# First layer's feed-forward: half-size products for the latent tokens, output products in groups of two, context part first at the end

## The chip, the cores and the metric

The kernel runs on one core of one Trainium2 chip. The metric is the device time of one execution in microseconds (us). A core has TensorE (PE in the rows; PEld is its weight load), VectorE (DVE), ScalarE (ACT), GpSimd (POOL) and the queue engine SP, which issues most DMAs. Each engine executes its instructions in the order in which they stand in its program.

## The reference, cut to what matters

Two layers over 512 latent tokens and 256 context tokens of width 1024, in float32. The change lies in the feed-forward of the first layer (`layer == 0`), which works on both kinds of tokens:

```python
def _swiglu(h, w_in, w_out):
    g, u = jnp.split(h @ w_in, 2, axis=-1)
    return (jax.nn.silu(g) * u) @ w_out
...
x = x + g1 * y
x = x + g2 * _swiglu(_rmsnorm(x, norm_w[layer, 1]) * (1.0 + sc2) + sh2, ffn_w_in[layer], ffn_w_out[layer])
if not last:
    ctx = ctx + cg1 * yc
    ctx = ctx + cg2 * _swiglu(_rmsnorm(ctx, norm_w[layer, 1]) * (1.0 + csc2) + csh2, ffn_w_in[layer], ffn_w_out[layer])
```

The hidden width is 2816, so `w_in` is 1024 x 5632 (2816 gate columns, 2816 up columns) and `w_out` is 2816 x 1024. The modulation vectors (`sc2`, `sh2`, `g2` and so on) come from `silu(c) @ ada_w[layer]`.

## The kernel before

**Numbers.** Every float32 product is made of three products of rounded halves. A value is split into a high part (a cast on ACT) and a low part (value minus high part, a subtraction on DVE), and a product is high x high + high x low + low x high, all added up in one PSUM bank. So each weight tile costs one ACT cast (`wh`, `xh`) and one DVE subtraction (`wl`, `xl`), and each activation tile likewise.

**Layout.** Activations lie with features on partitions and tokens along the free axis: columns 0 to 255 are context (`CTX`), 256 to 767 latent (`LAT`); `LA` and `LB` are the two halves of LAT. `xt` is the residual stream, `g0h`/`g0l` the normed input of the first feed-forward in its two parts, `h1h`/`h1l` the normed input of the second layer's attention.

**The first feed-forward** (`op_ffn`). The 2816 hidden features are 22 tiles of 128, taken two at a time (`pr`, 11 pairs). For a tile, gate and up columns are each multiplied with LAT in one go (matmuls of 512 columns into `pg` and `pu`) and with CTX (matmuls of 256 columns): 2 x 8 x 3 matmuls of either width. ACT takes the silu, DVE multiplies (`hfull`), ACT and DVE split the result (`fh`, `fl`). After pairs 2, 4, 6, 8 an output product (`outproj`, `pf`) follows over the four tiles before them; a last one takes the remaining six tiles, LAT first and then CTX, each followed by its norm. Each output bank is added to `xt` by one DVE instruction.

**The second feed-forward** (`op_ffn_seven`) works on latent tokens alone, and already uses seven half-size products instead of eight: the 1024 input features are cut in two halves, the gate/up columns are the second direction, the 512 tokens the third, and sums and differences of blocks are multiplied. It needs weight sums on DVE (`ws`), split like weights, forms of the activations (`hT`), and five DVE additions and subtractions of 256 columns per tile (`u`, `hfull`, `sq` from `pu`). Its rows show what such work costs.

**What sets the order.** `Flow` runs streams (generators) by modelled engine times and so writes out one program order. The streams are the main one (products, one after the other), `Weights` (loads of weights through three buffers `wr`, splits), norms, and `ada`: the modulation of later stages, which DVE computes as `acc` instructions of 1024 columns (two for each of 8 row blocks, or one where the context vector isn't needed). `op_ada` starts one such task after each of pairs 1 to 7; the first, (0, 40), gives the factors that every output product of this feed-forward needs. The row blocks of `ada_w` come through a ring of six buffers `aw`.

**Around it.** Ahead of the feed-forward stands the output product of the mixers (`op_out`, `pf` from `mh`, `ml`): 8 LAT products, the LAT norm, 8 CTX products, the CTX norm. A norm is `nsum` (PE sums the squares), `v` (DVE), a power on POOL, `nbc` (PE), then 8 multiplications on DVE with ACT and DVE or POOL behind them. After it stands the key projection of the attention (`pt`), latent chunks first, context chunks last.

Of the kernel before, what the change touches and what calls it, by code (L numbers as in the profile page):

```python
# [143 lines left out]
def kernel(ctx, tc, x, c, cx, c_ctx, ada_w, ada_b, norm_w, ffn_w_in, ffn_w_out, ab_w_in,  # L144
# [334 lines left out]
    F1 = {}  # L479


    class Weights:
# [8 lines left out]
        def plan(self, specs):  # L491

            for sp in specs:
                i = len(self.todo)
                if sp[0] in ("seven", "eight"):
# [39 lines left out]
        def seven(self, i, job):  # L535


            yield lambda: self.asked > job[1] and "pool" in F1
# [15 lines left out]
            def sums():  # L554
                return F1["pool"].tile([P, KT, P], F32, tag="ws", name=nm("ws"), bufs=3)

            x = [F1["pool"].tile([P, 12, P], F32R, tag=t, name=nm(t), bufs=2) for t in ("xh", "xl")]
# [16 lines left out]
            split("u", [t[:, 8:12] for t in x], u[:, 4:8])  # L574
            self.freed += 2
            self.ask()
            yield
# [4 lines left out]
            split("y", whl(), y)  # L582

# [154 lines left out]
    def ada_open():  # L738
        ada_ring["ctx"] = ExitStack()
        pool_ = ada_ring["ctx"].enter_context(tc.tile_pool(name="aw", bufs=6))  # L740
# [4 lines left out]
        for _ in range(6):  # L745
# [709 lines left out]
    def mixers_end():  # L1455
# [3 lines left out]
        ada_open()  # L1459

# [37 lines left out]
    op_out(ab_w_out[0], mixed, 0, 2, (LAT, CTX), op_norm(0, 1, "g0"), (32, 24))  # L1498
# [3 lines left out]
    def halves_ps(t):  # L1502
        return [t[:, 0:512], t[:, 512:1024]]

    def op_ffn(l, name, parts, ends, ada, then, last=None):

        acts = {}
        x_ = lambda: ready[name]

        def inproj(pr, ada):  # L1510
            def gen():
                th, tl = big([P, 2, NT], F32R, "fh"), big([P, 2, NT], F32R, "fl")
                acts[pr] = th, tl
                def evac(t, part, pg, pu):
                    a, b, mc = part
                    n = b - a
                    sg = t3("sq")
                    act.activation(sg[:, 0:n], pg[:, 0:n], AF.Silu)
                    fu = t3("hfull")
                    dve.tensor_tensor(fu[:, 0:n], pu[:, 0:n], sg[:, 0:n], ALU.mult)  # L1520
                    act.copy(th[:, t, a:b], fu[:, 0:n])
                    dve.tensor_tensor(tl[:, t, a:b], fu[:, 0:n], f(th[:, t, a:b]), ALU.subtract)

                for t in range(2):
                    first = pr == 0 and t == 0
                    u, ps = [], []
                    for i, part in enumerate(ends if first else parts):
                        a, b, mc = part
                        if first:
                            yield lambda: a in ready[name + "done"]  # L1530
                        for j in range(2):
                            if len(u) <= j:
                                u += yield from W.take(1)
                                ps.append([bank("pg") for _ in range(2)] if j == 0 else halves_ps(psum2("pu")))
                            yield from steps(ps[j][i][:, 0:b - a], pairs_feat(u[j], 0, *x_(), a, b), cut=24)
                            if part is (ends if first else parts)[-1]:
                                W.give(1)
                            if j:
                                evac(t, part, ps[0][i], ps[1][i])
                            flow.cur.t = 0.0  # L1540
                            yield
            specs = []
# [655 lines left out]
```

## Time and profile before

| | |
|---|---|
| median of the runs shown | 1776.29 us |
| profiled execution, its own time | 1777.82 us |
| span of the profiled execution | 1776.0 us |
| PE busy | 1721.4 us (97%) |
| DVE busy | 1136.9 us (64%) |
| ACT busy | 685.5 us (39%) |
| first feed-forward | about 545 to 1120 us of the span |
| second feed-forward | about 1400 to 1765 us of the span |

The time of the profiled execution is its span and 1.8 us around it. A busy PE is one with a matmul in its pipeline, so how quickly it works is read from the distance between the starts of matmuls. Durations of DVE instructions in the rows overlap those of their neighbours a little, so their cost in a row of instructions is also read from start to start.

### The profile page before, as it was taken

The numbers are of one execution on the slowest core, as the hardware profiler recorded it, in microseconds if no ns is written. First come the engines' busy times: TensorE is split into PE (matmuls) and PEld (weight loads), VectorE is DVE, ScalarE is ACT, GpSimd is POOL, SyncE is SP. The second block draws the span as 40 slices with busy tenths as digits, with TensorE's granted clock in tenths as the row PEclk, the third lists the DMA queues.
The fourth block names the chain that finished last, engine by engine and source line by source line (L and its number), as shares of the span: only waits on it lengthen the run. The fifth ranks groups of instructions, "written<-read, shape, count | busy, mean of one in ns | idle before, by whom it ended". The sixth has DMA issues, their size and how long they took to land.

```text
span 1776.0 us, 29522 instructions
## 1 busy us (share of the span) xinstructions
PE 1721.4 (97%) x11922; PEld 1528.9 (86%) x11922; DVE 1136.9 (64%) x2048; ACT 685.5 (39%) x1346; POOL 274.6 (15%) x271
## 2 busy tenths in 40 slices
PE   6899999999999999999999999898999999999998
PEld 5799899999878888888888888898666989999998
DVE  5845365756597376563544324869886687778785
ACT  4532344433325221212121123545776553444343
POOL 4211120201123000000000002426454300000000
PEclk8999899999999999999999999898999999999999
DMA  9511111011574264443542215322002623333335
GB/s 332 209 52 48 37 37 48 25 38 53 196 239 117 75 186 132 129 148 125 162 134 78 67 37 153 96 61 60 1 1 66 184 72 95 107 96 107 107 88 150
DMA packets 224556, 184.35 MB, mean 104 GB/s; under 512 B 7532, under 2 KB 206628, under 8 KB 224420
## 3 DMA queue, kind: packets, MB, share of 16 engines
q1 hardware_dynamic: 222468, 178.20, 32.9%
q10 hardware_dynamic: 1952, 4.27, 0.7%
q8 instruction: 94, 1.54, 0.4%
q14 instruction: 42, 0.34, 0.1%
HBM read 175.10 MB, written 7.34 MB: 103 GB/s over the span
## 4 chain that ended last, share of the span: by engine, by line
PE 84%; DVE 7%; ACT 3%; issue 3%; DMA 2%; POOL 1%; SPq 0%; POOLq 0%; ACTq 0%; DVEq 0%
PE pf L107 28%; PE pu L107 18%; PE pg L107 14%; PE pt L107 10%; PE sc L107 3%; PE ao L107 2%; PE mo L107 2%; PE atr L107 2%; PE ro L107 1%; DVE acc L107 1%; PE kv L107 1%; DVE wl L107 1%; PE me L107 1%; DMA wr<-in_ab_w_in_dram 1%; DVE hfull L107 1%
## 5 line engine op out<-in xcount | busy, mean ns | idle before, releaser
L107 ACT CAST wh<-wr 128x1024 fp32r<-128x1024 f32 (+1 forms) x186 | 188.2, 1012 | 345.7 <-PE pf L107 165.5
L107 DVE TENSOR_TENSOR wl<-wr,wh 128x1024 fp32r<-128x1024 f32 (+1 forms) x186 | 225.4, 1212 | 105.5 <-ACT wh L107 104.3
L107 POOL TENSOR_TENSOR nacc<-nacc,sq 128x256 f32<-128x256 f32 (+1 forms) x42 | 56.7, 1349 | 630.7 <-ACT sq L107 627.5
L107 DVE SCALAR_TENSOR_TENSOR xt<-pf,mod,xt 128x512 f32<-128x512 f32 (+1 forms) x160 | 97.7, 613 | 84.3 <-PE pf L107 83.8
L107 DVE TENSOR_TENSOR hfull<-pu,sq 128x512 f32<-128x512 f32 (+1 forms) x44 | 24.5, 557 | 149.9 <-PE pu L107 149.6
L107 PE MATMUL pf<-fh,wh 128*128 128x256 f32 (+1 forms) x352 | 119.3, 340 | 0.8 <-ACT wh L107 0.8
L107 PE MATMUL pf<-fl,wh 128*128 128x256 f32 (+1 forms) x352 | 118.5, 337 | 0.0
L107 PE MATMUL pf<-fh,wl 128*128 128x256 f32 (+1 forms) x352 | 118.0, 338 | 0.5 <-DVE wl L107 0.5
L107 PE MATMUL pf<-fu,wh 128*128 128x512 f32 (+1 forms) x448 | 116.2, 349 | 1.1 <-ACT fu L107 0.5
L107 PE MATMUL pu<-hT,wh 128*128 128x256 f32 x640 | 115.4, 280 | 0.0
L107 DVE SCALAR_TENSOR_TENSOR acc<-aw,cmod,acc 128x1024 f32<-128x1024 f32 x90 | 114.8, 1298 | 0.0
L107 PEld LDWEIGHTS pu<-hT,wh 128*128 128x128 f32 x640 | 97.8, 188 | 0.6 <-ACT hT L107 0.2
L107 PE MATMUL pu<-hT,wl 128*128 128x256 f32 x320 | 88.0, 281 | 1.4 <-DVE wl L107 1.4
L107 PE MATMUL pt<-wh,hh 128*128 128x256 f32 x288 | 84.2, 294 | 3.8 <-ACT hh L107 2.6
L107 PEld LDWEIGHTS pf<-fu,wh 128*128 128x128 f32 x448 | 76.8, 188 | 12.6 <-ACT fu L107 0.7
L107 PE MATMUL pt<-wl,hh 128*128 128x256 f32 x288 | 83.7, 292 | 0.0
L107 PE MATMUL pg<-g0h,wh 128*128 128x512 f32 (+1 forms) x220 | 82.1, 373 | 1.5 <-ACT sq L107 1.5
L107 POOL TENSOR_TENSOR aE<-aE,ast 128x512 f32<-128x512 f32 (+1 forms) x64 | 73.0, 1154 | 66.9 <-DVE ast L107 51.5
L107 PE MATMUL pg<-g0l,wh 128*128 128x512 f32 (+1 forms) x220 | 82.3, 374 | 0.0
L107 PE MATMUL pt<-wh,hl 128*128 128x256 f32 x288 | 82.2, 288 | 0.0
L107 PE MATMUL pu<-g0l,wh 128*128 128x512 f32 (+1 forms) x220 | 82.1, 373 | 0.0
L107 PE MATMUL pu<-g0h,wh 128*128 128x512 f32 (+1 forms) x220 | 81.9, 372 | 0.0
(382 smaller groups left out, 5169.2 us busy)
## 6 DMA issues: line engine op xcount, KB each, us to landing
wr<-in_ffn_w_in_dram SPq DMA_DIRECT2D x88, 512.0 KB, 3.9
aw<-in_ada_w_dram SPq DMA_DIRECT2D x84, 512.0 KB, 4.5
wr<-in_ab_w_in_dram SPq DMA_DIRECT2D x32, 512.0 KB, 4.3
wr<-in_ffn_w_out_dram SPq DMA_DIRECT2D x32, 512.0 KB, 4.7
wr<-in_ffn_w_out_dram SPq DMA_DIRECT2D x32, 384.0 KB, 3.6
wr<-in_ab_w_out_dram SPq DMA_DIRECT2D x16, 512.0 KB
wr<-in_attn_w_out_dram SPq DMA_DIRECT2D x16, 512.0 KB, 4.1
aw<-in_ada_w_dram SPq DMA_DIRECT2D x8, 768.0 KB
```

The lines of the kernel that those rows point to most:

```text
L107: r = fn(*a, **k)
```

## The change

The first feed-forward gets a function of its own, `op_ffn_first`.

- Its input product for the latent tokens is made of seven products of half size, as in the second layer; for the context tokens it stays as it was. Work goes by single tiles (`fi`, 22). The order in a tile is: b11, a context half, b21, t2, t3, n1, the other context half, n4, b22.
- The norm of LAT makes the forms that these products need (`norm_seven0`): b11 and b21 first, and t2, t3, n1, n4, b22 once the CTX part of the mixers' output product has been issued (`mixed`). The CTX norm starts after form n1.
- `Weights.seven` gets a third kind, "all", whose weights g, z, y and u are all 1024 wide; g and u go to a pool of their own (`F0`).
- Output products take two tiles each (nine groups of two, one of one, and the last of three). The last runs over CTX, LA, LB in turn, each with its norm behind it; the key and value projections behind it go by chunks 0, 1, 2 in place of 1, 2, 0.
- The `aw` ring holds three buffers in place of six, `ada` tasks start after tiles 0, 3, 6 and so on to 18, and the first has a shorter pause between its steps (1 us in place of 2, in `Flow`'s modelled time).

```diff
@@ Weights.seven
-            x = [F1["pool"].tile([P, 12, P], F32R, tag=t, name=nm(t), bufs=2) for t in ("xh", "xl")]
+            def xs_():
+                return [F["pool"].tile([P, F["rows"], P], F32R, tag=t, name=nm(t), bufs=2) for t in ("xh", "xl")]
+            x = xs_()
...
+            if job[2] == "all":
+                yield
+                yield spend((self.n_x, 1))
+                split("u", xs_(), u)
+                self.freed += 2
+                self.ask()
@@ ada_open
-        pool_ = ada_ring["ctx"].enter_context(tc.tile_pool(name="aw", bufs=6))
+        pool_ = ada_ring["ctx"].enter_context(tc.tile_pool(name="aw", bufs=3))
@@ norm_seven0
+        for q in range(4):
+            bb.append(big([P, 3, NL], F32, "bb"))
+            for k in range(2):
+                kk = 2 * q + k
+                dve.scalar_tensor_tensor(bb[q][:, k], xk(xt, kk, a, b), amod[0][:, 1, kk, 0:1], bcs, ALU.mult, ALU.mult)
+                act.activation(bb[q][:, k], bb[q][:, k], AF.Identity, bias=mod[0][:, 24 + kk, 0:1])
+            two(("b11", "b21")[q // 2], q % 2, bb[q][:, 0:2, 0:256])
+        done0.update(("b11", "b21"))
...
+        yield lambda: "mixed" in done0
+        for name in ORDER0[2:]:
+            for q, (b11, b21, b12, b22, t2) in enumerate(four):
+                if name == "t3":
+                    dve.tensor_tensor(b12, b12, b22, ALU.subtract)
+                if name == "n4":
+                    dve.tensor_tensor(b21, b21, t2, ALU.subtract)
+                two(name, q, {"t2": t2, "t3": b12, "n1": b11, "n4": b21, "b22": b22}[name])
+            done0.add(name)
+            yield
@@ op_ffn_first.inproj
+                product(bank_a, u["g"], 0, "b11")
+                act.copy(m1, bank_a)
...
+                if fi:
+                    bank_e = psum("pc", "mx")
+                    yield from context(0)
...
+                product(bank_a, u["g"], 4, "b21", start=False)
...
+                product(bank_b, u["z"], 0, "t2")
+                dve.tensor_tensor(u23[:, 0], bank_b, m1, ALU.subtract)
...
+                product(bank_d, u["y"], 0, "t3")
+                dve.tensor_tensor(u23[:, 1], bank_d, u23[:, 0], ALU.add)
...
+                product(bank_c, u["y"], 4, "n1")
+                W.give(1)
+                cc = t3("hfull")
+                dve.tensor_tensor(cc[:, 256:512], u23[:, 1], bank_c, ALU.subtract)
...
+                product(bank_d, u["u"], 4, "n4", start=False)
...
+                dve.tensor_tensor(cc[:, 0:256], bank_d, u23[:, 0], ALU.add)
...
+                product(bank_c, u["z"], 4, "b22", start=False)
+                W.give(1)
+                dve.tensor_tensor(m1, bank_c, u23[:, 0], ALU.subtract)
+                act.activation(m1, m1, AF.Silu)
+                dve.tensor_tensor(cc, cc, keep, ALU.mult)
+                act.copy(t[:, 0, NCX:NT], cc)
+                dve.tensor_tensor(t[:, 1, NCX:NT], cc, f(t[:, 0, NCX:NT]), ALU.subtract)
...
+            op(gen, [("all",) + columns(0, fi)])
+            if ada and fi % 3 == 0:
                 l_, t0 = ada.pop(0)
+                op_ada(l_, t0, on_pe=(), gap=5.0 if l_ else 1.0, cols=1 if l_ and t0 >= 16 else 2)
@@ op_ffn_first.outproj
             if end:
+                for part in (CTX, LA, LB):
                     op(lambda part=part: gen((part,)), specs)
                     then(part)
...
+        groups = {fi: (fi - 2, fi - 1) for fi in range(2, 12, 2)}
+        groups[11] = (10,)
+        groups.update((fi, (fi - 2, fi - 1)) for fi in range(13, 20, 2))
+        groups[NF - 1] = (NF - 3, NF - 2, NF - 1)
@@ op_tok, keys and values of the attention
-    op_tok(wat[:, D:D + 256], h1, (1, 2, 0), evac_nr(1, lambda c2: None if c2 == 0 else 2 * c2 - 2, post_k, kdone.add),
+    op_tok(wat[:, D:D + 256], h1, (0, 1, 2), evac_nr(1, lambda c2: None if c2 == 0 else 2 * c2 - 2, post_k, kdone.add),
```

Whole program, matmuls of the two products of the first feed-forward: before, 1584 of 512 columns (1056 of the input product, 528 of the output product) and 1584 of 256 columns (the same two parts); now, 456 of 512 columns and 3576 of 256 columns (2904 of the input product, 672 of the output product).

DVE, between the LAT norm and the first products of the feed-forward; `xt` adds a CTX output bank of the mixers, `bb` are the normed latent blocks and `g` the low parts of the forms. Before:

```order
L107 SCALAR_TENSOR_TENSOR g0l_5545<-hfull_5631,mod_173,g0h_5542 128x512
L107 SCALAR_TENSOR_TENSOR xt_4891<-pf_5804,mod_173,xt_4891 128x256
L107 TENSOR_TENSOR wl_5841<-wr_5796,wh_5839 128x1024
L107 SCALAR_TENSOR_TENSOR hfull_5640<-xt_4890,amod_175,nbc_5617 128x512
L107 SCALAR_TENSOR_TENSOR xt_4891<-pf_5845,mod_173,xt_4891 128x256
L107 TENSOR_TENSOR wl_5909<-wr_5802,wh_5907 128x1024
```

Now, at the same place:

```order
L107 SCALAR_TENSOR_TENSOR xt_4891<-pf_5823,mod_173,xt_4891 128x256
L107 TENSOR_TENSOR bb_5640<-bb_5640 128x2x256
L107 TENSOR_TENSOR wl_5911<-ws_5878,wh_5910 128x1024
L107 TENSOR_TENSOR wl_5927<-ws_5879,wh_5926 128x1024
L107 TENSOR_TENSOR bb_5632<-bb_5648,bb_5632 128x512
L107 TENSOR_TENSOR bb_5632<-bb_5632,bb_5648 128x2x256
L107 TENSOR_TENSOR g_907_5653<-bb_5648,g_905_5645 128x512
L107 SCALAR_TENSOR_TENSOR bb_5656<-xt_4891,amod_175,nbc_5627 128x512 x2
L107 TENSOR_TENSOR ws_6107<-wr_5805,wr_5957 128x512
L107 TENSOR_TENSOR ws_6107<-wr_5957 128x512
L107 TENSOR_TENSOR g_934_5856<-bb_5632,g_907_5653 128x512
```

Sums of blocks (`bb`), sums of weights (`ws`) and their splits stand there now, among the multiplications of the norm; the low part of the last quarter of b21 comes after them.

DVE, ahead of the first output product: `acc` belongs to the task (0, 40), `wl` from `wr` is the low part of the output weights, `xt` from `pf` the first addition. Before:

```order
L107 TENSOR_TENSOR fl_6425<-hfull_6622,fh_6424 128x512
L107 TENSOR_TENSOR wl_6656<-wr_6416,wh_6654 128x1024
L107 TENSOR_TENSOR hfull_6690<-pu_6595,sq_6688 128x256
L107 TENSOR_SCALAR acc_6714<-aw_6489,cmod 128x1024
L107 TENSOR_TENSOR wl_6710<-wr_6519,wh_6708 128x1024
L107 TENSOR_SCALAR acc_6716<-aw_6489,cmod 128x1024
L107 TENSOR_TENSOR fl_6425<-hfull_6690,fh_6424 128x256
L107 STREAM_TRANSPOSE row_6704<-row_6703 128x256
```

Now:

```order
L107 SCALAR_TENSOR_TENSOR acc_6115<-aw_6171,cmod,acc_6115 128x1024
L107 TENSOR_TENSOR hfull_6280<-pu_6228,u_981_6123 128x256
L107 TENSOR_TENSOR wl_6347<-ws_6283,wh_6346 128x1024
L107 TENSOR_TENSOR xl_6411<-wr_6246,xh_6410 128x1024
L107 SCALAR_TENSOR_TENSOR acc_6117<-aw_6171,cmod,acc_6117 128x1024
L107 TENSOR_TENSOR fu_6121<-sq_6350,fu_6121 128x256
L107 SCALAR_TENSOR_TENSOR acc_6115<-aw_6188,cmod,acc_6115 128x1024
L107 TENSOR_TENSOR keep_6122<-pu_6267,u_981_6123 128x256
L107 TENSOR_TENSOR wl_6434<-wr_6248,wh_6432 128x1024
```

The task (0, 40) stands among the splits of the second and third tile, and the low part of the first output weights (`wl_6434`) stands behind most of it.

PE at the start of the first output product, where `wl_6434` is read (`pu`, `pg`: banks of the tiles; `ada`: column sums of the finished `acc`). Before, the product of pairs 0 and 1, between the products of a later pair:

```order
L107 MATMUL pg_6560<-g0h_5544,wh_6412 128x256
L107 MATMUL pg_6560<-g0l_5547,wh_6412 128x256
L107 MATMUL pg_6560<-g0h_5544,wl_6414 128x256
L107 MATMUL pf_6720<-fh_5879,wh_6585 128x512
L107 MATMUL pf_6720<-fl_5880,wh_6585 128x512
L107 MATMUL pf_6720<-fh_5879,wl_6587 128x512
L107 MATMUL pu_6595<-g0ch_5918,wh_6515 128x256
```

Now, the product of tiles 0 and 1, among the products of the third tile (`pg` is its product with b11):

```order
L107 MATMUL pu_6451<-g_943_5905,wh_6346 128x256
L107 MATMUL pu_6451<-g_942_5900,wl_6347 128x256
L107 MATMUL pf_6541<-fu_5861,wh_6432 128x512 x2
L107 MATMUL pf_6541<-fu_5861,wl_6434 128x512
L107 MATMUL ada_6210<-acc_6115,ones 32x256 x4
L107 MATMUL pg_6358<-g_903_5637,xh_6263 128x256 x2
L107 MATMUL pg_6358<-g_903_5637,xl_6264 128x256
```

The first output product comes after two tiles in place of four, and the sums of the task (0, 40) stand right behind its first rows. Between the LAT norm's `nsum` and the row that reads `wl_6434` stand 432 matmuls of 256 columns, which are 144 of the mixers' CTX output product, 264 of the first two tiles and 24 of the third.

## Rows read from the trace of the kernel before

**Rows 1.** The page's part 1: busy us, share, instructions, by engine.
```profile
PE 1721.4 (97%) x11922; PEld 1528.9 (86%) x11922; DVE 1136.9 (64%) x2048; ACT 685.5 (39%) x1346; POOL 274.6 (15%) x271
```

**Rows 2.** The page's part 4: the chain that ended last, by engine.
```profile
PE 84%; DVE 7%; ACT 3%; issue 3%; DMA 2%; POOL 1%; SPq 0%; POOLq 0%; ACTq 0%; DVEq 0%
```

**Rows 3.** Windows, first and second feed-forward: length, busy by engine, clock, DMA share, GB/s.
```profile
545.00:1110.00 565.00, 562.67 (x3241) 485.96 (x3241) 287.38 (x369) 134.63 (x202) 19.52 (x17) 1.00 0.38 116
1500.00:1740.00 240.00, 238.89 (x1741) 225.08 (x1739) 189.21 (x286) 99.77 (x146) 0.00 (x0) 1.00 0.33 98
```

**Rows 4.** Timeline of PE, starts of matmuls of 512 and of 256 columns.
```profile
1080.17 0.40 PE L107 MATMUL pf<-fh,wh 128*128 128x512 f32 x1
...
1098.70 0.39 PE L107 MATMUL pf<-fh,wl 128*128 128x512 f32 x1
...
1108.97 0.28 PE L107 MATMUL pf<-fl,wh 128*128 128x256 f32 x1
...
1111.33 0.28 PE L107 MATMUL pf<-fh,wh 128*128 128x256 f32 x1
```

**Rows 5.** Timeline of DVE, instructions that stand close behind each other.
```profile
655.44 0.75 DVE L107 TENSOR_SCALAR acc<-aw,cmod 128x1024 f32<-128x1024 f32 x1
656.11 1.22 DVE L107 TENSOR_TENSOR wl<-wr,wh 128x1024 fp32r<-128x1024 f32 x1
...
671.40 2.47 DVE L107 SCALAR_TENSOR_TENSOR acc<-aw,cmod,acc 128x1024 f32<-128x1024 f32 x2
673.79 0.48 DVE L107 SCALAR_TENSOR_TENSOR xt<-pf,mod,xt 128x256 f32<-128x256 f32 x1
674.18 1.21 DVE L107 TENSOR_TENSOR wl<-wr,wh 128x1024 fp32r<-128x1024 f32 x1
...
1681.00 0.69 DVE L107 TENSOR_TENSOR xl<-wr,xh 128x512 fp32r<-128x512 f32 x1
1681.61 2.36 DVE L107 TENSOR_TENSOR wl<-ws,wh 128x1024 fp32r<-128x1024 f32 x2
1683.88 0.75 DVE L107 SCALAR_TENSOR_TENSOR xt<-pf,mod,xt 128x512 f32<-128x512 f32 x1
1684.54 0.68 DVE L107 TENSOR_TENSOR ws<-ws,wr 128x512 f32<-128x512 f32 x1
...
1704.21 0.41 DVE L107 TENSOR_TENSOR hfull<-pu,u 128x256 f32<-128x256 f32 x1
1704.55 0.41 DVE L107 TENSOR_TENSOR u<-pu,m 128x256 f32<-128x256 f32 x1
```

**Rows 6.** Timeline of PE and of DVE at the LAT norm ahead of the feed-forward.
```profile
529.73 1.05 PE L107 MATMUL nsum<-cst,nacc 128*128 128x1 f32 x8
...
534.78 0.15 DVE L107 TENSOR_SCALAR v<-nsum 128x4 f32<-128x4 f32 x1
```

**Rows 7.** Waits of PE, 525 to 580 us.
```profile
PE pf L107 <- DVE xt L107: 2.0, 2, 1.6
```

**Rows 8.** Windows: ahead of the first feed-forward, and at the second one's forms (columns as in rows 3).
```profile
534.80:557.40 22.60, 22.60 (x167) 20.71 (x166) 19.43 (x29) 14.56 (x23) 12.45 (x11) 1.00 0.71 201
1430.00:1440.00 10.00, 9.29 (x76) 8.86 (x75) 9.97 (x18) 8.26 (x17) 0.00 (x0) 1.00 0.01 2
```

**Rows 9.** Windows behind the first feed-forward (columns as in rows 3).
```profile
1120.00:1130.00 10.00, 8.01 (x52) 7.38 (x51) 5.72 (x9) 5.08 (x8) 6.04 (x6) 0.83 0.48 145
1130.00:1140.00 10.00, 7.75 (x51) 7.55 (x50) 8.50 (x21) 4.59 (x10) 1.64 (x1) 0.82 0.01 2
1140.00:1150.00 10.00, 9.67 (x69) 9.70 (x70) 7.36 (x11) 3.83 (x6) 4.18 (x3) 0.83 0.00 1
1150.00:1160.00 10.00, 10.00 (x87) 10.00 (x87) 7.86 (x14) 5.63 (x10) 1.65 (x1) 1.00 0.33 105
```

**Rows 10.** Waits of PE, 1116 to 1160 us.
```profile
PE pt L107 <- DVE sq L107: 2.6, 1, 2.6
```

**Rows 11.** DMA issues, 545 to 1110 us: count, KB, median us to landing.
```profile
aw<-in_ada_w_dram SPq DMA_DIRECT2D x50, 512.0 KB, 3.9
```

More of the change, by code (lines that the diff above doesn't have):

```diff
@@ L477, in spend @@
         return cond
-    F1 = {}
+    F0, F1 = {}, {}
     class Weights:
@@ L535, in seven @@
         def seven(self, i, job):
-            yield lambda: self.asked > job[1] and "pool" in F1
+            F = F0 if job[2] == "all" else F1
+            yield lambda: self.asked > job[1] and "pool" in F
             yield spend((self.n_x, 1))
@@ L744, in ada_open @@
         ada_ring["todo"] = ada_ring["plan"]
-        for _ in range(6):
+        for _ in range(3):
             ada_ask()
@@ L1459, in mixers_end @@
         ada_open()
+        F0["ctx"] = ExitStack()
+        F0["pool"] = F0["ctx"].enter_context(tc.tile_pool(name="f0", bufs=1))
+        F0["rows"], F0["sums"] = 8, 2
     op_do(mixers_end)
@@ L1497 @@
     mixed = lambda: (lambda k, a, b: mh[k // 2][:, k % 2, a:b], lambda k, a, b: ml[k // 2][:, k % 2, a:b])
[L1498 to L1505, printed above, removed]
-        acts = {}
-        x_ = lambda: ready[name]
-        def inproj(pr, ada):
-            def gen():
[L1512 to L1542, printed above, removed]
-            for t in range(2):
-                c0 = 256 * pr + P * t
-                specs += [wfeat(ffn_w_in[l, :, c:c + P]) for c in (c0, DFF + c0)]
-            op(gen, specs)
-            if ada and pr >= 1:
-                l_, t0 = ada.pop(0)
-                op_ada(l_, t0, on_pe=(), gap=5.0 if l_ else 2.0, cols=1 if l_ and t0 >= 16 else 2)
-        def outproj(prs):
-            nk = 2 * len(prs)
-            r0 = 256 * prs[0]
-            ncol = 256 if nk == 4 else P
-            end = prs[-1] == DFF // 256 - 1
-            bh = lambda k, a, b: acts[prs[k // 2]][0][:, k % 2, a:b]
-            bl = lambda k, a, b: acts[prs[k // 2]][1][:, k % 2, a:b]
-            specs = [(ffn_w_out[l, r0:r0 + P * nk, ncol * s:ncol * s + ncol], nk, ncol) for s in range(D // ncol)]
@@ new lines, in norm_ctx0, with norms0, run, columns @@
+    def norm_ctx0():
+        yield lambda: "n1" in done0
+        yield from norm_mod(0, 1, ctx0(0), ctx0(1), CTX, done0)
+    def norms0(part):
+        def run():
+            flow.add(norm_seven0() if part is LAT else norm_ctx0(), 3, "norm")
+            if part is CTX:
+                done0.add("mixed")
+        op_do(run)
+    op_out(ab_w_out[0], mixed, 0, 2, (LAT, CTX), norms0, (32, 24))
+    def columns(l, fi):
+        return tuple(wfeat(ffn_w_in[l, :, c:c + P]) for c in (P * fi, DFF + P * fi))
@@ L1567, in gen @@
                             a, b, mc = part
-                            ps = (bank if end and last else wide_bank)("pf")
+                            ps = wide_bank("pf")
                             yield from steps(ps[:, 0:b - a], pairs_feat(u, P * t, bh, bl, a, b, nk))
@@ L1837, in reload1 @@
         F1["pool"] = ctx.enter_context(tc.tile_pool(name="f1", bufs=1))
+        F1["rows"], F1["sums"] = 12, 3
         xt = [big([P, 3, NL], F32, "xt") for _ in range(3)]
@@ L2063, in gen @@
                 yield from rest(fi, fi > PLAIN + 1)
-            op(gen, [("seven",) + columns(fi)])
+            op(gen, [("seven",) + columns(1, fi)])
         def outproj(fs):
@@ L2098, in outproj @@
                 op(lambda: gen((LAT,)), specs)
-        op(plain, [("eight",) + columns(fi) for fi in range(PLAIN)])
+        op(plain, [("eight",) + columns(1, fi) for fi in range(PLAIN)])
         for fi in range(PLAIN, NF):
```

153 lines of the change are left out of this document (126 added, 27 removed).

## The prediction

> **What bounds the kernel now.** I read the page's totals first: TensorE is busy 97% of the span, VectorE 64% [rows 1], and the chain of work that ended last lies 84% on TensorE [rows 2]. So the kernel gets shorter by fewer matmul cycles, and longer by whatever makes TensorE wait. The windows over the stage come next: in the first feed-forward TensorE is busy 562.67 of 565 us at full clock, VectorE 287.38, which is 51% [rows 3]. The second feed-forward is already made of seven products, and there VectorE is busy 189.21 of 240 us, 79%, while TensorE still has 238.89 of 240 [rows 3]. This kind of work can therefore run without TensorE waiting, once it is under way. Whether it also starts without waiting is the main question, and for that the timeline of the two engines around the LAT norm is needed [rows 6], with the windows there and where the second layer's forms are made [rows 8].
>
> **Matmuls: what the change saves.** Durations of matmuls overlap, so I take the distance of starts. From 1080.17 to 1098.70 us there are 80 matmuls of 512 columns: 0.2317 us each. From 1108.97 to 1111.33 there are 20 of 256 columns: 0.118 each [rows 4]. A half-size one costs 2% more than half of a full one. The change removes 1584 of the one and 1584 of the other, 367.0 + 186.9 = 553.9 us, and brings 456 and 3576, 105.7 + 422.0 = 527.6 us. TensorE's own work gets **26.3 us** less, all on the bounding engine.
>
> The paces of rows 4 speak against a rule of the Trainium skill, "TensorE: Matmul & The Clock Gate", section "Back-to-back issue gap", by which a sustained stream of weight load and matmul takes about 81 ns at 128 columns and 131 ns at 512. An estimate between these two for 256 columns is 98 ns; by it the change would remove 362.7 us and bring 410.2, a kernel 47 us slower. The trace has 231.7 ns at 512, which is near that section's formula for a single matmul instead (columns / 2.4 + 2.5 ns, 216), so I leave that rule out.
>
> **VectorE over the stage.** Prices from start to start [rows 5]: a 1024-wide subtraction 1.135 us (two from 1681.61 to 1683.88), a 512-wide one 0.61, a 512-wide multiply-add 0.66, a 256-wide one 0.39, a 256-wide addition 0.34, an `acc` 1.195 (two from 671.40 to 673.79), the first `acc` of a task 0.67. The stage gains some 47 wide subtractions (53 us), 88 weight sums (54), five 256-wide operations in each of 22 tiles (37), 104 additions to `xt` because groups are smaller (52), and 22 operations for forms (13): about 209 us. Then VectorE has 287 + 209 = 496 of about 540 us, 92%. A steady tile needs some 16 us of VectorE against 23.9 of TensorE, and the rest is `acc` (about 91 us). That leaves a margin after the start, and none to catch up quickly.
>
> **The start of the stage, the largest cost.** The order shows that from the LAT norm's `v` up to `wl_6434`, the low part of the first output weights, VectorE has 17 wide subtractions (19.3), 36 operations of 512 columns (22.0), 8 multiply-adds of 512 (5.3) and 22 of 256 (8.6), 14 of 256 (4.8), 11 `acc` (13.1) and two first ones (1.3), and 0.6 of small ones: **75.0 us**. `v` starts at 534.78 [rows 6], so VectorE is there at 609.8 at the earliest. TensorE, free behind `nsum` at 529.73 + 1.05 = 530.8 [rows 6], has up to the same point 432 matmuls of 256 columns (51.0), two of 512 and some small ones (1.7): 583.5 us if nothing stopped it. It stands 4 us ahead at the beginning because VectorE is behind already. Hence TensorE waits 26.3 us on the way if VectorE never pauses. How near to that it comes: 9.97 of 10 us in the second layer's forms, but 19.43 of 22.6 (86%) in the norm here [rows 8]. I take 95%, nearer to the first, since there as here VectorE works through forms and splits while TensorE waits: 78.9 us, a wait of 30.2. At 86% it is 38. Before has 2.0 us of waits of its own in this stretch [rows 7], so the cost is **+28**, between +24 and +36. The edit of the order that causes it is that form sums, weight sums, wide splits and the first `ada` task all fall into these 75 us; without the `acc` the wait would be 14 us shorter.
>
> **Later in the stage.** Up to the evacuations of the ninth tile VectorE has 221.7 us since `v` and TensorE 214 since `nsum`, by the same counts and prices. So the lag grows no further there if VectorE keeps above 95%, and from there on it shrinks. For small waits beyond that I put **+2** (0 to 10). Pauses of TensorE can also cost clock: behind the stage, stretches with pauses run at a granted clock of 0.83 and one full 10 us later at 1.00 [rows 9]. For the start of the stage I put **+2** for that, and more in a rival.
>
> **The end of the stage.** Now, when the last product is done, the norm and first keys follow with a dip: 52 matmuls in 1120 to 1130 us, 69 in 1140 to 1150, against 87 at full clock [rows 9], of which one wait of 2.6 us on VectorE [rows 10]. That is a loss of 9 to 12 us, part of it by the clock (0.82 to 0.83). After the change the CTX and LA norms lie under the passes over LA and LB (24 passes of nine half-size matmuls in all, 1.06 us each), and key chunks 0 and 1 (48 matmuls of 256 columns, 5.7 us) stand in front of what needs the LB norm. That norm has the same chain, VectorE, GpSimd, TensorE and 8 multiplications, so a wait of some 5 us and a dip of the clock stay. I put **-4** (0 to -8).
>
> **Edits costed at nothing.** The `aw` ring of three: a block lands 3.9 us after it is asked for [rows 11], and between the ask and the use stand at least 11 us of VectorE's work; without this cover each of the 50 blocks [rows 11] could cost up to 3.9 us, but on VectorE's queue and not on TensorE's. The DMA traffic rises by the wider loads, and its share of 0.38 [rows 3] leaves room.
>
> **Sum.** -26.3 + 28 + 2 + 2 - 4 = +1.7 us against the profiled execution, 1777.8, which is 1779.5. That execution lies 1.5 above the median shown (1776.29), so the forecast is **1778 us**. About 2% (35 us) is what a measurement of this kernel can tell from no change. With VectorE at 100% and -8 at the end the sum is -10 (1766); with 36 at the start and 10 of later waits it is +20 (1796).
>
> **Rivals.**
> - *The saving comes through.* If VectorE's backlog at the start is hidden (work standing earlier than I read it, or TensorE given other work while it waits), -26.3 and -4 are left: 1746, and 1741 with the whole end gained. For it speaks that the second feed-forward runs so [rows 3]; against it that the counts at the start leave 26 us between two queues that execute in order.
> - *VectorE stays the bound* up to the ninth tile, the slower side. Its queue is full, and each pause in it, for a PSUM bank that TensorE hasn't finished, is passed on. At 85%, 221.7 us become 261, VectorE is there at 796 and TensorE's work alone at 745: a wait of 51, with clock losses 1801. Above 2% slower it comes out where the wait passes 63 us, at a busy share below 0.81. The 86% of the norm [rows 8] speak for it, the 79% at which the second feed-forward needs no waits [rows 3] against.
> - *The clock falls in the VectorE-bound stretch.* Three 10-us rows behind the stage lose 1.7 us each to the clock [rows 9]; over a stretch of 80 us at the start that is up to 14 us, which gives 1792. The Trainium skill ("TensorE: Matmul & The Clock Gate", section "A second HAM failure mode: psum-queue depth-cycling") describes the same: short pauses between groups of matmuls swing the clock and cost throughput. The rows behind the stage agree, those of the second feed-forward, at 1.00, show no such pauses.
> - That the change doesn't do what it says is out: the order has the counts of matmuls used above.
>
> **How the numbers follow.** Chances: the forecast 0.58, saving through 0.18, VectorE bound 0.12, clock 0.12. The forecast and its bounds take 1762 to 1796; the range reaches to most of the second case and to the third's time: 1750 to 1802. Faster by over 2% (under 1741) needs the second case with all of the end: 0.05. Slower by over 2% (over 1812) needs the third with a share below 0.81, or both losses: 0.07. Within 2%: 0.88.
>
> **What would show it.** Right: half-size matmuls 0.118 us apart in the tiles; between 535 and 615 us VectorE without gaps, waits of TensorE on VectorE (`g`, `wl`, `u`) of 25 to 35 us in total, and after some 750 us hardly any; the stage within 5 us of its old length. Wrong: half-size products further apart than 0.12 us; VectorE with gaps while TensorE waits for it; waits that go on through the whole stage, or on `aw` blocks; a granted clock below 1.00 in the steady tiles.

## The result and the profile after

The changed kernel takes **1819.88 us** (median; its runs lie between 1817.89 and 1821.68) against 1776.44 us of the kernel before in the same comparison: a ratio of 1.0246, 95% interval 1.0226 to 1.0266. It is 43 us slower; 1778 us was forecast, and the range ended at 1802.

The page's part 1 of the changed kernel, in the columns of [rows 1]:

```profile
PE 1717.5 (94%) x12786; PEld 1563.7 (86%) x12786; DVE 1339.5 (74%) x2424; ACT 751.7 (41%) x1463; POOL 283.5 (16%) x279
```

TensorE's share has fallen from 97% to 94% in a longer span, and VectorE has 203 us more. Of the chain of work that ended last, more lies on VectorE (part 4 of the page, as in [rows 2]):

```profile
PE 73%; DVE 15%; DMA 5%; issue 3%; ACT 3%; POOL 1%; SPq 0%; POOLq 0%; DVEq 0%; ACTq 0%
```

To see where the time went I count the **lost time** of TensorE in a stretch: its length less what its matmuls take at the paces of [rows 4] (0.2317 us for 512 columns, 0.118 for 256, other widths in proportion), with every matmul of the timeline counted. Waits and matmuls at a lower clock both count as lost. The stretches end at the same work in either kernel: the last input product of the stage (at 1066 us before, 1118 now) and the first score product of the attention (1191 and 1234).

| | before | now | more | forecast |
|---|---|---|---|---|
| matmuls of the stage | | | -26.3 | -26.3 |
| lost, 520 to 640 us (start) | 6.0 | 42.1 | +36 | +28 and +2 |
| lost, 640 us to the last input product (middle) | -0.5 | 17.4 | +18 | +2 |
| lost, from there to the first score product (end) | 15.6 | 31.3 | +16 | -4 |
| sum | | | +43 | +1.7 |

The measured difference is 43, so the count closes within 1 us. In the middle, where nothing is in the way, half-size matmuls run at the pace forecast. Windows, in the columns of [rows 3]:

```profile
1040.00:1060.00 20.00, 20.00 (x172) 20.00 (x171) 10.33 (x15) 7.84 (x12) 0.00 (x0) 1.00 0.42 131
```

172 matmuls in 20 us are 0.116 us each.

**The start.** Windows from 550 us on, against [rows 8]:

```profile
550.00:560.00 10.00, 5.30 (x36) 4.60 (x36) 10.00 (x15) 6.70 (x12) 3.96 (x3) 0.93 0.56 158
560.00:570.00 10.00, 4.60 (x17) 3.93 (x17) 10.00 (x18) 6.83 (x12) 6.11 (x2) 0.50 0.01 2
570.00:580.00 10.00, 6.58 (x42) 6.37 (x43) 8.12 (x15) 4.09 (x7) 2.64 (x1) 0.72 0.00 0
...
600.00:610.00 10.00, 7.22 (x48) 7.01 (x48) 10.00 (x14) 3.76 (x6) 0.00 (x0) 0.83 0.51 163
610.00:620.00 10.00, 5.64 (x34) 4.18 (x32) 10.00 (x12) 1.51 (x3) 0.00 (x0) 0.83 0.49 161
```

VectorE is busy 10.00 of 10 us in four of these rows, while TensorE is busy 4.60 to 7.22. There are two holes, not one: around 560 (the forms) and around 610 (the first modulation task); in the two rows between them, left out here, TensorE is busy 9.82 and 9.06 us. In the first the clock is granted at 0.50, its lower level, so that 17 matmuls take 4.60 us. Over the whole way from `nsum` to the first output product, and from there to 640 us:

```profile
530.80:617.40 86.60, 65.06 (x465) 60.79 (x466) 80.40 (x119) 40.98 (x67) 18.63 (x9) 0.86 0.38 115
617.40:640.00 22.60, 21.00 (x141) 17.56 (x142) 16.15 (x25) 7.03 (x12) 0.00 (x0) 0.79 0.43 135
```

TensorE is idle for 21.5 and 1.6 us of them, VectorE busy for 80.40 of 86.60, 93%. TensorE's longest waits on that way:

```profile
PE nbc L107 <- POOL rs L107: 5.7, 1, 5.7
PE pg L107 <- ACT g L107: 3.5, 2, 2.9
PE pf L107 <- DVE keep L107: 2.8, 1, 2.8
PE pu L107 <- DVE u L107: 2.8, 1, 2.8
```

**The middle.** The waits of TensorE from 640 to 1118 us, the longest kind, and the window over the stretch:

```profile
PE pf L107 <- DVE xt L107: 8.6, 9, 2.5
```

```profile
640.00:1118.00 478.00, 466.61 (x3478) 437.12 (x3477) 383.60 (x571) 142.80 (x212) 0.00 (x0) 1.00 0.36 111
```

VectorE is busy 383.60 of 478 us, 80%, about the share at which the second feed-forward ran without waits [rows 3]. TensorE's idle time in the window is 11.4 us; the rest of the 17.4 are delays between starts too short to show as idle time. One of the waits, in the timelines of VectorE and, below, of TensorE:

```profile
752.08 0.48 DVE L107 SCALAR_TENSOR_TENSOR xt<-pf,mod,xt 128x256 f32<-128x256 f32 x1
752.47 0.69 DVE L107 TENSOR_TENSOR fu<-hfull,fu 128x512 fp32r<-128x512 f32 x1
753.07 2.48 DVE L107 SCALAR_TENSOR_TENSOR acc<-aw,cmod,acc 128x1024 f32<-128x1024 f32 x2
755.46 0.75 DVE L107 SCALAR_TENSOR_TENSOR xt<-pf,mod,xt 128x512 f32<-128x512 f32 x1
```

```profile
756.27 1.03 PE L107 MATMUL pf<-fu,wh 128*128 128x512 f32 x2 [2.50 <-DVE xt L107]
```

From one addition to `xt` to the next pass 3.4 us, 3.0 of them other work, two `acc` among it; a bank of two tiles is filled in 6 x 0.2317 = 1.4 us, and TensorE has none left.

**The end.** Windows, against [rows 9], and the longest waits behind 1118 us, against [rows 10]:

```profile
1120.00:1130.00 10.00, 6.97 (x60) 6.79 (x59) 10.00 (x19) 5.98 (x13) 4.89 (x6) 1.00 0.39 127
1130.00:1140.00 10.00, 8.99 (x50) 8.78 (x50) 4.55 (x10) 3.00 (x7) 3.78 (x4) 0.66 0.38 118
...
1170.00:1180.00 10.00, 3.26 (x28) 3.07 (x27) 5.01 (x13) 4.01 (x9) 5.37 (x5) 0.82 0.01 4
1180.00:1190.00 10.00, 7.11 (x46) 7.14 (x47) 5.27 (x10) 3.75 (x7) 3.37 (x3) 0.67 0.01 2
```

```profile
PE pt L107 <- DVE hfull L107: 9.6, 1, 9.6
PE pf L107 <- DVE xt L107: 5.0, 3, 3.0
```

The half-width passes come too fast for VectorE (10.00 of 10 us in the first row), and behind them TensorE waits 9.6 us for the LB norm (`hfull`); the longest wait before was 2.6 us [rows 10]. Not all of the 31.3 us are waits: between 1118 and 1190 us TensorE is idle for 18.4 us, and the granted clock, 0.83 on the mean there and 0.66 to 0.82 in three of these rows, accounts for about the rest (0.17 of 72 us, 12 us).

### The profile page after: what moved, and what is told of

Its sections match the earlier page's. It is cut to its first block, busy times and chain, and to the rows that moved or that the text cites. A ratio compares the mean times of both kernels' runs of the same rounds, so it can differ in the third digit from the quotient of the medians.

```text
span 1819.1 us, 31730 instructions
## 1 busy us (share of the span) xinstructions
PE 1717.5 (94%) x12786; PEld 1563.7 (86%) x12786; DVE 1339.5 (74%) x2424; ACT 751.7 (41%) x1463; POOL 283.5 (16%) x279
## 4 chain that ended last, share of the span: by engine, by line
PE 73%; DVE 15%; DMA 5%; issue 3%; ACT 3%; POOL 1%; SPq 0%; POOLq 0%; DVEq 0%; ACTq 0%
PE pf L107 24%; PE pu L107 13%; PE pt L107 10%; PE pg L107 7%; PE pc L107 5%; DVE acc L107 3%; PE sc L107 3%; DVE wl L107 3%; DMA wr<-in_ffn_w_in_dram 2%; PE ao L107 2%; PE mo L107 2%; PE atr L107 2%; DVE xt L107 2%; DMA aw<-in_ada_w_dram 1%; DVE hfull L107 1%
## 5 line engine op out<-in xcount | busy, mean ns | idle before, releaser
L107 PE MATMUL pf<-fu,wh 128*128 128x256 f32 (+1 forms) x1200 | 302.7, 343 | 18.6 <-DVE xt L107 13.9
L107 PEld LDWEIGHTS pf<-fu,wh 128*128 128x128 f32 x1200 | 206.1, 193 | 47.7 <-DVE xt L107 15.4
L107 PE MATMUL pf<-fu,wl 128*128 128x256 f32 (+1 forms) x600 | 202.8, 339 | 1.1 <-DVE wl L107 1.1
L107 DVE SCALAR_TENSOR_TENSOR xt<-pf,mod,xt 128x256 f32<-128x256 f32 (+1 forms) x264 | 154.4, 604 | 32.4 <-PE pf L107 32.0
L107 PE MATMUL pu<-g,wh 128*128 128x256 f32 x704 | 131.9, 284 | 2.6 <-ACT g L107 2.1
L107 PE MATMUL pc<-g,xh 128*128 128x256 f32 x704 | 128.4, 280 | 0.6 <-ACT keep L107 0.5
L107 PEld LDWEIGHTS pf<-fu,wl 128*128 128x128 f32 x600 | 116.0, 193 | 14.5 <-DVE wl L107 2.0
L107 PEld LDWEIGHTS pu<-g,wh 128*128 128x128 f32 x704 | 110.3, 191 | 4.8 <-ACT g L107 2.3
L107 PEld LDWEIGHTS pc<-g,xh 128*128 128x128 f32 x704 | 108.6, 188 | 1.5 <-ACT keep L107 0.7
L107 DVE TENSOR_TENSOR wl<-ws,wh 128x1024 fp32r<-128x1024 f32 x84 | 102.3, 1222 | 6.8 <-ACT wh L107 6.2
```

The lines of the kernel that those rows point to most:

```text
L107: r = fn(*a, **k)
```

## The experiments

Lost time in us by the same three stretches (their ends at the same work as above), median, and ratio to the kernel before in the same comparison with its interval; 0.001 of it is 1.8 us. Lost times and times agree within 5 us or so.

| kernel | start | middle | end | median us | ratio (95%) |
|---|---|---|---|---|---|
| before | 6.0 | -0.5 | 15.6 | 1776.44 | 1 |
| changed | 42.1 | 17.4 | 31.3 | 1819.88 | 1.0246 (1.0226 to 1.0266) |
| acc_first_thin | 28.6 | 17.9 | 31.3 | 1810.34 | 1.0194 (1.0177 to 1.0211) |
| acc_rest_thin | 40.3 | 3.2 | 32.6 | 1809.85 | 1.0190 (1.0175 to 1.0205) |
| end_as_before | 41.9 | 14.5 | 20.5 | 1805.56 | 1.0167 (1.0152 to 1.0182) |
| before_new_end | 5.9 | -0.5 | 23.1 | 1784.08 | 1.0049 (1.0033 to 1.0064) |
| before_groups_two | 5.9 | 6.6 | 14.8 | 1783.35 | 1.0033 (1.0021 to 1.0045) |
| ctx_nbc_later | 39.2 | 13.7 | 30.6 | 1814.84 | 1.0209 (1.0193 to 1.0224) |
| first_ada_early | 19.3 | 17.5 | 31.1 | 1803.48 | 1.0144 (1.0128 to 1.0161) |
| sums_pool | 41.4 | 18.1 | 33.9 | 1824.96 | 1.0266 (1.0250 to 1.0281) |
| early_oldend | 21.1 | 17.7 | 22.1 | 1795.08 | 1.0105 (1.0089 to 1.0122) |
| acc_spread | 40.6 | 10.6 | 32.4 | 1816.80 | 1.0225 (1.0210 to 1.0241) |
| groups_three | 42.8 | 8.9 | 31.7 | 1815.06 | 1.0219 (1.0202 to 1.0236) |
| all_four | 19.4 | 5.5 | 21.6 | 1781.82 | 1.0036 (1.0023 to 1.0049) |
| all_four_pe | 15.1 | 7.1 | 20.5 | 1785.18 | 1.0042 (1.0027 to 1.0057) |
| all_four_nbc | 19.7 | 5.2 | 23.6 | 1784.95 | 1.0048 (1.0034 to 1.0062) |
| all_four_both | 16.5 | 6.5 | 21.9 | 1787.35 | 1.0057 (1.0044 to 1.0069) |
| before_ada_pe | 3.7 | -0.4 | 14.1 | 1776.31 | 0.9999 (0.9990 to 1.0008) |

**Who fills VectorE at the start and in the middle: acc_first_thin and acc_rest_thin.** An `acc` past a task's first step works on 64 columns, in the first task or in the six later ones; the rest of the sums is left out:

```diff
-                        z = dve.scalar_tensor_tensor(acc[i], u, s_, acc[i], ALU.mult, ALU.add)
+                        m = 64 if thin else D
+                        z = dve.scalar_tensor_tensor(acc[i][:, 0:m], u[:, 0:m], s_, acc[i][:, 0:m], ALU.mult, ALU.add,
+                                                     as_if=D)
```

(`as_if` keeps the modelled cost; the order in the traces still differs from the changed kernel's in a number of places.)

> The changed kernel, but the steps 1 to 7 of the first modulation task (0, 40) work on 64 of their 1024 columns (14 instructions; the rest of the sums is left out). Theory V, VectorE's queue bounds the start of the stage: some 14 us less VectorE work ahead of the first output product, TensorE's loss between 520 and 640 us falls from about 42 to about 25 us, the whole kernel 14 to 18 us shorter (1802 to 1806 us). Rival G, the loss at the start comes from the norm and form chain itself, to which the task adds nothing: 1816 to 1820 us.

> The changed kernel, but steps 1 to 7 of the six later modulation tasks work on 64 of 1024 columns (56 instructions, about 56 us of VectorE; the rest of the sums is left out). Theory V, the waits of the output products on VectorE between 640 and 1120 us (20 us lost) come from bursts in which acc, splits and additions to xt fall together: the loss there falls to 5 us or less, the kernel is at about 1803 us (1800 to 1808). Rival G, output banks that are filled in 1.4 us and have to be emptied one by one are the cause, with or without acc: 1815 to 1820 us.

Each takes loss away in its own place and hardly elsewhere: the first 13.5 of 42.1 us at the start, the second 14.2 of 17.4 in the middle. The second hole is gone with the first task thin; the first hole stays. Windows of acc_first_thin:

```profile
560.00:580.00 20.00, 10.62 (x51) 9.59 (x50) 18.12 (x31) 10.92 (x18) 9.87 (x2) 0.57 0.00 1
...
600.00:620.00 20.00, 20.00 (x171) 18.72 (x170) 15.19 (x32) 8.61 (x13) 0.00 (x0) 1.00 0.73 237
```

By the lost time theory V holds for the second hole and for the middle; what is left at the start, 28.6 us, lies ahead of 600 us, about half of it in the first hole. The times fell by 9 and 10 us and missed both expectations (14 to 18, and 12 to 20); why less came through isn't shown.

**The end: end_as_before and before_new_end.** The order of the last output product and of the key and value chunks, undone in the changed kernel, and put alone into the kernel before:

```diff
-                for part in (CTX, LA, LB):
+                for part in (LAT, CTX):
...
-    op_tok(wat[:, D + 256:D + 512], h1, (0, 1, 2), evac_v1, after=v_after1)
+    op_tok(wat[:, D + 256:D + 512], h1, (1, 2, 0), evac_v1, after=v_after1)
```

(the key chunks alike, with the norm that each waits for)

> The changed kernel with the end of the stage as before: the last output product over all latent tokens and then the context, key and value chunks 1, 2, 0. Theory E, the new order at the end costs: 10 to 15 us shorter than the changed kernel (1805 to 1810 us). Rival S, the last group of three tiles covers only half as much of VectorE's splits and norms as the six tiles before, in either order: 1816 to 1824 us.

> The kernel before with the new end alone: last output product of six tiles over context, first and second half of the latent tokens, key and value chunks 0, 1, 2. Theory E, the new order at the end costs: 8 to 15 us longer than before (1785 to 1791 us). Rival S, with six tiles under each pass the norms are covered: 0 to 6 us shorter (1770 to 1776 us).

Theory E holds from both sides: 14 us (1805.56 against 1819.88) come back in the one, 8 us (1784.08 against 1775.83 in the same comparison) are lost in the other, where the passes are twice as long. Its longest wait behind 1063 us is the one of the changed kernel again:

```profile
PE pt L107 <- DVE hfull L107: 8.1, 1, 8.1
```

The lost time at the end falls by 10.8 and rises by 7.5 us; with 2.9 us less in the middle of the first, that is in line with the times. The order of the passes and that of the chunks weren't undone apart.

**Groups of two by themselves: before_groups_two.** In the kernel before:

```diff
-            if pr >= 2 and pr % 2 == 0 and pr < npr - 2:
-                outproj([pr - 2, pr - 1])
+            if 2 <= pr < npr - 2:
+                for q in (0, 1) if pr == 2 else (pr - 1,):
+                    outproj([q])
```

> The kernel before with output products over two tiles in place of four (the last one over six as it was), everything else as it was. VectorE gets 64 more additions to xt there (some 32 us) in a stage in which it is busy 51%. Theory V, output banks wait only because VectorE's queue is full: no change, 1773 to 1779 us. Rival G, short groups make TensorE wait for banks by themselves: 10 to 20 us longer (1786 to 1796 us).

Between the two: 6 us longer, and the middle loses 7 us that it didn't before, with VectorE far from full (247.32 of 420 us in 640 to 1060 us). So some of the 18 us in the middle belong to short groups as such.

**The context norm's nbc: ctx_nbc_later.**

```diff
@@ norm_ctx0
-        yield lambda: "n1" in done0
@@ norm_mod
-        bcs = yield from rms_bc((ps2[:, a // P:b // P], a // P))
+        bcs = yield from rms_bc((ps2[:, a // P:b // P], a // P), (lambda: 'b22' in done0) if mc and w_ and not l else None)
@@ rms_bc
-        yield
+        yield wait
...
+            order(m_, flow.main if wait else None)
```

> The changed kernel, but nbc of the context norm ahead of the stage stands some 26 matmuls later on TensorE, and its v three places earlier on VectorE, so that the power on GpSimd (5.9 us) runs beside products. Theory N, of the 42 us lost at the start some 6 are this wait, and a few more the clock that falls in it: 4 to 9 us shorter (1811 to 1816 us). Rival F, the low parts of the forms are late in any case and TensorE waits for them instead: within 2 us (1818 to 1822 us).

5 us shorter, within the range of theory N, but not by its mechanism: the lost time falls by 3 us at the start and by 4 in the middle, and the wait for GpSimd has only moved. TensorE now waits at the norm's `nsum`, for an addition on GpSimd, as its waits from 525 to 645 us show:

```profile
PE nsum L107 <- POOL nacc L107: 7.0, 1, 7.0
```

The power itself takes longer still, in the timeline of GpSimd:

```profile
564.93 10.12 POOL L107 TENSOR_TENSOR rs<-v,mhalf 128x2 f32<-128x2 f32 x1 [2.08 <-DVE v L107]
```

What the moved order does in the middle isn't shown.

**The first task out of the way: first_ada_early.**

```diff
-                    op_ada(l, adas.pop(0), on_pe=(0, 1))
+                    t0 = adas.pop(0)
+                    op_ada(l, t0, on_pe=range(KT) if t0 == 40 else (0, 1))
...
-    op_out(ab_w_out[0], mixed, 0, 2, (LAT, CTX), norms0, (32, 24))
+    op_out(ab_w_out[0], mixed, 0, 2, (LAT, CTX), norms0, (32, 24, 40))
```

> The changed kernel, but the first modulation task (0, 40) runs ahead of the stage, among the context products of the mixers, and its sums on TensorE (8 rounds of about 0.45 us) in place of VectorE. Theory V: the loss between 520 and 640 us falls as far as with the thin task (42 to 29 us) or further, less some 3 us of TensorE work: 1806 to 1811 us. Rival D, its 4 MB come into a stretch in which the DMA share is already 0.72 to 0.85, and weights come later: 1816 us or more.

Better than expected: 23 us less lost at the start and 16 us less in time, since TensorE now has 48 small matmuls more. The window of the first hole of this kernel:

```profile
560.00:580.00 20.00, 13.88 (x81) 11.66 (x81) 20.00 (x37) 12.56 (x22) 2.56 (x3) 0.83 0.16 52
```

81 matmuls at a mean clock of 0.83, in place of 59 (17 and 42) at 0.50 and 0.72 in the changed kernel: the first hole is smaller too, the wait for the power on GpSimd in it is 2.5 us, and the clock falls less. What in the moved order does that was not tried apart. The DMA (busy 0.91 of its time in 530 to 560 us) cost one wait of TensorE on a block of `aw`, 1.9 us.

**Weight sums on GpSimd: sums_pool.**

```diff
-            dve.tensor_tensor(y[:, 0:4], g[:, 0:4], u[:, 0:4], ALU.add)
+            eng = pool if job[2] == "all" and self.alls > 3 else dve
+            eng.tensor_tensor(y[:, 0:4], g[:, 0:4], u[:, 0:4], ALU.add)
```

(and the three other sums alike)

> The changed kernel, but the four weight sums of a tile run on GpSimd in place of VectorE from the fifth tile on (72 instructions, some 43 us of VectorE's time). Theory V: the loss between 640 and 1118 us falls from 19 to 8 us or less, the kernel is at 1805 to 1812 us. Rival P, GpSimd is slow (a 256-wide addition takes 1 to 4 us in this trace) and slows VectorE beside it, so that the weights come late: 1820 us or more.

The rival was right in the time: 4 to 5 us longer, and the middle loses no less (18.1 against 17.4) although 72 sums have left VectorE. Groups by form of VectorE, 640 to 1110 us, first of sums_pool:

```profile
L107 DVE SCALAR_TENSOR_TENSOR acc<-aw,cmod,acc 128x1024 f32<-128x1024 f32 x56 | 86.1, 1548 | 0.1
L107 DVE TENSOR_TENSOR wl<-wr,wh 128x1024 fp32r<-128x1024 f32 x17 | 25.0, 1469 | 1.3 <-ACT wh L107 0.5
```

and of the changed kernel:

```profile
L107 DVE SCALAR_TENSOR_TENSOR acc<-aw,cmod,acc 128x1024 f32<-128x1024 f32 x56 | 71.3, 1284 | 0.0
L107 DVE TENSOR_TENSOR wl<-wr,wh 128x1024 fp32r<-128x1024 f32 x17 | 20.8, 1222 | 0.3
```

With additions on GpSimd beside it the same `acc` takes 1548 in place of 1284 ns.

**Together: early_oldend, acc_spread, groups_three, all_four.** The first joins first_ada_early and end_as_before; all_four joins the other two to it.

```diff
-                op_ada(l_, t0, on_pe=(), gap=5.0 if l_ else 1.0, cols=1 if l_ and t0 >= 16 else 2)
+                op_ada(l_, t0, on_pe=(), gap=8.0 if l_ else 1.0, cols=1 if l_ and t0 >= 16 else 2)
...
-        groups = {fi: (fi - 2, fi - 1) for fi in range(2, 12, 2)}
-        groups[11] = (10,)
-        groups.update((fi, (fi - 2, fi - 1)) for fi in range(13, 20, 2))
+        groups = {fi: (fi - 3, fi - 2, fi - 1) for fi in range(3, 19, 3)}
+        groups[19] = (18,)
```

> The changed kernel with two parts undone or moved: the first modulation task ahead of the stage with its sums on TensorE (16 us shorter by itself), and the end as before (14 us shorter by itself). The two lie 500 us apart. If start and end are separate losses, they add up: 1788 to 1791 us. Rival C, TensorE that comes earlier to the middle of the stage finds VectorE in the same backlog and gives part back: 1794 us or more.

> The changed kernel with a pause of 8 in place of 5 us (modelled time) between the steps of the six later modulation tasks, so that the same 70 acc spread over more of the 72 us between two tasks. Theory V-burst, what is lost between 640 and 1118 us is lost where acc come one upon another ahead of additions to xt: loss 19 to 11 us or less, 1808 to 1814 us. Rival V-sum, VectorE is too full on the whole: 1817 to 1822 us.

> The changed kernel with output products over three tiles in place of two (one group of one near the end, the last three as they were): 56 additions to xt fewer, and each bank filled for 2.1 us in place of 1.4. By the 7 us that groups of two in place of four cost in the kernel before, and VectorE fuller here: loss between 640 and 1118 us 19 to 8 us, 1807 to 1812 us. Rival, the waits come from acc alone, since without acc they were gone: 1816 to 1820 us.

> All four together: first modulation task early and on TensorE, the end as before, groups of three, the later tasks spread. If the losses are separate: 1820 - 16 - 14 - 10 - 3 = 1777 us, the time of the kernel before within 5 us; the saving of 26 us in matmuls then only pays for what is left of the start (about 13 us more than before) and the middle. Rival: 1785 us or more, if VectorE's backlog simply moves.

early_oldend misses its mark by 4 us: start and end each lose 2 us more than in the single runs, so part is given back, though not in the middle, where rival C had it. Spreading the `acc` takes 7 us from the middle, as theory V-burst had it (10.6 is left, 11 or less was expected), but only 3 to 4 from the time. It does so with VectorE no less full (383.23 of 470 us in 640 to 1110 us, 82%, against 80%): what counts is how the `acc` fall, not the share. Groups of three take 9 us from the middle, but 5 from the time. all_four comes to 1781.82 us, 6 us behind the kernel before: of the 43 us it has 37 back. Its lost time is 25 us more than before's (46.5 against 21.1), and the early task adds 48 small matmuls; together they eat the 26.3 us of matmuls that the change saves.

**What is left at the start: all_four_pe, all_four_nbc, all_four_both, before_ada_pe.** The tasks (0, 32) and (0, 24) ahead of the LAT norm wholly on TensorE too (`op_ada(l, adas.pop(0))` in `op_out`), nbc later, both, and the first of these in the kernel before.

> all_four, and the two modulation tasks (0, 32) and (0, 24) ahead of the LAT norm wholly on TensorE too (12 rounds of 0.45 us there, some 28 us off VectorE). Theory B, VectorE stands behind at v because of these acc: v 4 to 5 us earlier, the loss between 520 and 640 us 19 to 12 us or less, the kernel 1776 to 1779 us. Rival F, the forms alone make TensorE wait: 1782 to 1787 us, longer by the added TensorE work.

> all_four with the context norm's nbc later on TensorE, as in ctx_nbc_later. Only 2.5 us of wait on the power on GpSimd are left in all_four. Theory N: 1778 to 1780 us. Rival F: within 1 us of all_four (1781 to 1783 us).

> all_four with both edits. If B and N both hold: 1773 to 1776 us, the time of the kernel before or a little less. If F holds: 1781 us or more.

> The kernel before with the tasks (0, 32) and (0, 24) wholly on TensorE. VectorE is not the bound there but for 2 us of waits: 1775 to 1781 us (5 us of TensorE work more, up to 4 us of waits less). If VectorE's backlog already costs the kernel before, it is 1772 us or less.

None is faster than all_four, and the kernel before doesn't change. With the tasks on TensorE the start loses 4 us less, but TensorE has 64 matmuls more to do. The stretch of the forms in all_four_pe:

```profile
520.00:540.00 20.00, 20.00 (x165) 15.67 (x168) 9.22 (x13) 6.63 (x10) 5.35 (x4) 1.00 0.81 248
...
560.00:580.00 20.00, 12.12 (x69) 10.63 (x68) 20.00 (x36) 10.88 (x19) 3.19 (x3) 0.85 0.18 53
```

VectorE now has time to spare ahead of the norm (9.22 of 20 us), and still is busy 20.00 of 20 when the forms are made, with TensorE at 12.12. So rival F comes nearest: theory B's 12 us or less weren't reached (15.1), and what remains at the start, some 9 us more than before, is lost where the forms are made. That the forms alone cost it is argued, not shown. Of VectorE's 20 us in the last row some 6.5 are weight sums and their splits, TensorE waits there 3.1 us for GpSimd in front of `nsum` and some 3.6 for the forms (`g`), and the clock is 0.85; no run leaves the forms out.

## Why the prediction was wrong

- **The matmuls (-26.3)** were right: the pace is 0.116 to 0.118 us, and the sum of losses and savings closes within 1 us with this term. In all_four they pay for nearly all that is still lost. The other sum for the matmuls in the prediction, 47 us slower, lies near the measured 43 by chance: it needs 0.098 us for a half-size matmul.
- **The wait for VectorE at the start (+28)** was right in mechanism and nearly in size. `wl_6434` was forecast for 613.7 us; in the timelines of VectorE and of TensorE it runs from 616.98, and the product from 617.22:

```profile
616.98 1.23 DVE L107 TENSOR_TENSOR wl<-wr,wh 128x1024 fp32r<-128x1024 f32 x1
```

```profile
617.22 1.19 PE L107 MATMUL pf<-fu,wh 128*128 128x512 f32 x2 [2.85 <-DVE keep L107]
```

  VectorE was busy 93% of the way, where 95% was assumed. From `nsum` up to that point TensorE loses 32.8 us, against 3.4 before from the same point on to 640 us.
- **The clock at the start (+2)** was too small: the forecast put it among the rivals at up to 14. From 530.8 to 640 us 38 us are lost, and 23 of them are idle time in the windows; most of the rest are matmuls at a lower granted clock, 0.86 on the mean up to the first output product and 0.79 behind it, where hardly anything is waited for. Together the start cost 36 in place of 30. That the power on GpSimd in front of `nbc` (5.7 us) is one of these waits was not seen; ctx_nbc_later only moved the wait, and 3 us less were lost at the start.
- **"For small waits beyond that I put +2 (0 to 10)"** is the first step that failed: 18 us. The step before it compared busy shares: the second feed-forward needs no waits at 79%, so a margin was read into the steady tiles. The share is 80% here as well, and 17 us are lost. What decides is what stands in VectorE's queue between two additions to `xt`: two `acc` and a split or sum are 3 us or more, a bank of two tiles is full after 1.4. acc_rest_thin (3.2 us lost), acc_spread (10.6, at a share of 82%), groups_three (8.9) and before_groups_two (7 us from short groups alone) show both halves of this. The rival "VectorE stays the bound" had a full queue too, but passing on VectorE's own pauses for banks that TensorE hasn't finished, as one wait up to the ninth tile; here TensorE waits for banks that VectorE hasn't emptied, through the whole middle.
- **The end (-4, 0 to -8)** is the second, with the wrong sign: +16. The forecast let 5.7 us of key products cover the LB norm and put the wait at 5; it is 9.6, and half-width passes wait for VectorE as well, 5.0 us in three waits. By the two experiments on it the new order costs 8 us in the kernel before and 14 in the changed one.
- **The edits costed at nothing**: no wait of TensorE on `aw` blocks appears among the waits of the stage. That the ring of three costs nothing was not tried by itself.

The middle and the end are 36 us off together, and their sizes were taken without a count of what VectorE's queue holds there, which had been made for the start.

## What to carry to other kernels

When work is moved from TensorE to VectorE, count VectorE's queue between two evacuations against the time in which a bank is filled, everywhere in the stage; a busy share of 80% doesn't answer it. Shorter groups and half-width passes shorten that time, other tasks on the same engine fill that queue, and here leaving one of them out gave back 5 to 14 us. And look at what is left uncovered at the end of a stage: here TensorE's longest wait there was for the last of three norms.

## What the runs showed of the hardware

The power on GpSimd for the context norm (`rs`, 128 x 2 elements) took 5.90 us in the row of VectorE additions at the start of the changed kernel, and 0.71 for the same norm in the kernel before, in the timelines of GpSimd, the changed kernel's first:

```profile
566.74 5.90 POOL L107 TENSOR_TENSOR rs<-v,mhalf 128x2 f32<-128x2 f32 x1 [3.89 <-DVE v L107]
```

```profile
557.58 0.71 POOL L107 TENSOR_TENSOR rs<-v,mhalf 128x2 f32<-128x2 f32 x1 [1.35 <-DVE v L107]
```

That is eight times as long for the same operation, and in sums_pool VectorE is slowed in turn (1548 against 1284 ns for an `acc`). The Trainium skill, "SBUF — State Buffer", section "SBUF: two separate sides", says that VectorE operations with two SBUF inputs and GpSimd operations that read SBUF use one pair of ports, which one of them holds for a whole instruction while the other stands still. Both measurements agree with it in kind. How long GpSimd stands still doesn't follow from them: the 5.90 us lie beside nine VectorE instructions, in ctx_nbc_later the power took 10.12 us, and in first_ada_early, where VectorE is as full, 1.09. No run shows what decides it.

The modulation sums are cheap on TensorE: of the first task in first_ada_early, three of the eight rounds on the timeline of TensorE are one row, 24 matmuls in 1.50 us (the other five take 0.64 us each):

```profile
541.64 1.50 PE L107 MATMUL ada<-aw,cmod 128*32 128x256 f32 x24
```

On VectorE one round is two `acc`, 2.4 us.
